# Fewer places for each expert of a mixture of experts, and one more second product that holds its weights

## The chip, the cores and the metric

The kernel runs on one core of a Trainium2 chip. The metric is the device time of one execution in microseconds. Before the change it was 4212.13 us, the median of three runs (4209.02 to 4219.26).

## The reference

One encoder layer over 2048 tokens of width 1024, with 16 meta tokens in front that take part in attention and are dropped at the end. Two groups of attention heads are mixed and added to the tokens with a layer norm. Then each token goes to 4 of 32 experts:

```
logits = h @ w_router + b_router
top_val, top_idx = lax.top_k(logits, 4); gates = softmax(top_val)
# rows sorted by expert, group_sizes = bincount of the choices
hgu = lax.ragged_dot(xs, w_gate_up, group_sizes) + b_gate_up[e]   # 1024 -> 2048
act = clamped_swiglu(hgu)                                         # 1024
out = lax.ragged_dot(act, w_down, group_sizes) + b_down[e]        # 1024 -> 1024
moe = segment_sum(out * gates, tok)
h = layernorm(2**0.25 * h + moe)
```

8192 rows (2048 tokens by 4) are spread over the experts as the router's logits have it, so the experts differ in size. All data are float32.

## The kernel before

The kernel first computes attention and the mixed tokens, then the router, and then runs the experts. This change bears on the experts alone; they begin at about 1646 us.

**Places by rank.** The kernel counts the rows of each expert on the chip and sorts the experts by their counts. The program is fixed, so each rank r has a fixed number of places, `CAPS[r]`, from 512 for the largest to 128 for the smallest five; the expert itself is looked up by rank when its weights are loaded (`job`, L1831). All places are computed, whether a row stands in them or not. What goes beyond an expert's places is done after the 32 jobs by a loop `tc.For_i(0, ni)`, one expert piece of 256 places (`OB`) a turn; `ni` is computed on the chip (`leftover`, L1406) and may be 0.

**A job.** `order` sets the jobs in pairs, a large rank and a small one: 1, 26, 2, 25, 3, 24, 4, 23, 5, 22, 6, 21, 7, 20, 8, 19, 9, 18, 10, 31, 11, 30, 12, 29, 13, 28, 14, 27, 15, 17, and then 16 and 0. The places of a job are cut into tiles of up to 128 rows (`j.tb`). Rows are gathered from HBM by an indirect DMA on GpSimd's queue (`rows`, L1514), turned by TensorE and split into a high and a low part (`turns`, L1522); this is done for the next job during the second product of the one before. Weights come in 12 pieces of 1024 KB a job, 8 of the first product and 4 of the second, each split by ScalarE (high, L1472) and VectorE (low, L1478) some pieces ahead.

Products take three terms: high by high, low by high and high by low. There are three modes, by places n:

- over 248 ("w3"): the first product (`up_ws`, L1580) holds weights and streams n columns; 8 steps, 2 halves, 24 matmuls each (L1590, L1591, L1595);
- 129 to 248 ("w2"): high and low rows stand side by side, so a pass with the high weights streams 2n columns (L1593) and one with the low weights n (L1595), 16 matmuls a half;
- up to 128 ("ts"): rows are held and weights are streamed, 256 columns a matmul (L1560, L1562).

The second product has two forms. `down_ts` (L1765) holds the rows: 4 pieces by tiles, 24 matmuls of 256 columns each (L1773); ScalarE scales the result by the gate into `y`. `down_ws` (L1788) holds the weights and streams the job's columns: 8 blocks of 24 matmuls of n columns (L1803), or 16 of 2n and n columns in w2 (L1799); the result comes out turned, so it is copied, turned back by TensorE tile by tile (L1816) and scaled (L1820). `thin(n)` says which form a job has. When the last piece of a tile's `y` is there, `rows_out` (L1626) adds its rows into the sums `acc_d` in HBM with an indirect scatter on GpSimd's queue. The tool that sets waits makes each scatter wait for the one before.

**The end.** During the last job (rank 0) the kernel normalises all tokens: `norms` (L1689) reads pairs of 128 sums from `acc_d` through SP's queue, takes statistics on VectorE, the root on GpSimd, scales on ScalarE, and shifts on VectorE and GpSimd. Its steps are put between the last job's by the list `TICKS`, in each engine's order. The first read comes in step 0 of the last job and its statistics between steps 1 and 2. The last job's own rows are normalised after their second product (`sums`, `rows_end`), for which GpSimd gathers their sums behind its share of the norms.

Of the kernel before, what the change touches and what calls it, by code (L numbers as in the profile page):

```python
# [48 lines left out]


OB = 256
CAPS = [512, 476, 444, 424, 376, 348, 332, 316, 316, 312, 312, 304, 300, 300, 292, 284,
        264, 244, 244, 232, 216, 212, 208, 200, 200, 188, 160, 128, 128, 128, 128, 128]
MAXI = 8192 // OB + NE

ROOT_BITS = float(0x5f3759df - 2 ** 30 - 2 ** 22)
# [4 lines left out]

def thin(n):

    return 128 < n <= 216 or 256 < n <= 332 or 384 < n < 460


def tables():
# [865 lines left out]
def project(k, a, pre):  # L933
# [16 lines left out]
    with ExitStack() as ctx:  # L950
# [42 lines left out]
        def iota(t, step, base, part):  # L993
            nc.gpsimd.iota(t, pattern=[[step, t.shape[1]]], base=base, channel_multiplier=part,
                           allow_small_or_imprecise_dtypes=True)
# [4 lines left out]
        iota(k.r.spare, 0, S + 1, 1)  # L1000
        for r, c in enumerate(CAPS):
            nc.gpsimd.memset(k.r.crow[:, r:r + 1], float(c))
# [379 lines left out]
def experts(k, a, out):  # L1382
    tc, nc = k.tc, k.nc
    with ExitStack() as ctx:
# [446 lines left out]
        def job(p):  # L1831
            while len(jobs) <= p:
                r = order[len(jobs)]
                j = K()
                j.r, j.n = r, CAPS[r]
                j.mode = "ts" if j.n <= 128 else "w2" if j.n <= 248 else "w3"
                j.dw, j.last = thin(j.n), len(jobs) == NE - 1
                j.e = nc.sync.value_load(k.r.eid[0:1, r:r + 1], min_val=0, max_val=NE - 1)
                j.off = nc.sync.value_load(k.r.off[0:1, r:r + 1], min_val=0, max_val=(NE - 1) * TS)
                j.bias, j.biasa, j.early = k.r.bias[:, :, r], biasa[:, :, r], []  # L1840
                start(j)
                jobs.append(j)
            return jobs[p]
# [214 lines left out]
```

## Time and profile before

| | |
|---|---|
| median of 3 runs | 4212.13 us (4209.02 to 4219.26) |
| profiled execution | 4220.97 us, its span 4219.1 us |
| mean granted TensorE clock | 0.981 of full speed |
| TensorE busy | 4058.6 us (96%) |
| VectorE / ScalarE / GpSimd busy | 2870.7 (68%) / 2386.2 (57%) / 615.9 (15%) |
| HBM read / written | 519.92 / 109.19 MB |

The profile is one execution. Busy times are averages over attention, router, experts and the end, which have different limits. Matmuls overlap, and their ends are modelled; where the price of one matmul matters, the stretch from one start to another is divided by their number.

### The profile page before, as it was taken

How to read it: one execution, taken by the hardware profiler on the slowest of the kernel's cores; microseconds unless marked ns; L12 is line 12 of the kernel's file. 1: busy time of each engine (PE TensorE's matmuls, PEld its weight loads, DVE VectorE, ACT ScalarE, POOL GpSimd, SP SyncE). 2: the span in 40 equal slices, each digit the busy share in tenths (PEclk: the TensorE clock that was granted, in tenths of full speed). 3: DMA queues.
4: the chain of work that ended last, by engine and by line, in shares of the span. 5: the costliest groups of instructions: out<-in, count | busy, mean ns of one | idle time of the engine just before them, and what ended most of it. 6: DMA issues, size and time to landing. Idle time of an engine off the chain costs nothing.

```text
span 4219.1 us, 63411 instructions
## 1 busy us (share of the span) xinstructions
PE 4058.6 (96%) x24294; PEld 3677.9 (87%) x24294; DVE 2870.7 (68%) x4629; ACT 2386.2 (57%) x3847; POOL 615.9 (15%) x547
## 2 busy tenths in 40 slices
PE   8999999999999997999999999999999999999995
PEld 6887777888887776999999999999999999999985
DVE  8876888888887885455554654665655566665665
ACT  5454888866665333455464555565555566665542
POOL 1010011100000341010010100111110011100156
PEclk9999999999999998999999999999999999999997
DMA  5332201111102535465565665766666677776653
GB/s 195 125 124 83 76 28 43 32 37 46 38 29 90 170 112 165 117 199 159 157 195 157 194 188 165 221 194 178 205 200 192 202 243 233 239 222 206 213 189 143
DMA packets 574203, 633.40 MB, mean 150 GB/s; under 512 B 68464, under 2 KB 519664, under 8 KB 573856
## 3 DMA queue, kind: packets, MB, share of 16 engines
q1 hardware_dynamic: 545600, 551.90, 40.6%
q0 software_dynamic: 26528, 75.21, 7.5%
q8 instruction: 195, 3.19, 0.3%
q10 hardware_dynamic: 1760, 2.11, 0.1%
q14 instruction: 120, 0.98, 0.1%
HBM read 519.92 MB, written 109.19 MB: 149 GB/s over the span
## 4 chain that ended last, share of the span: by engine, by line
PE 51%; DMA 5%; DVE 2%; POOL 2%; issue 1%; ACT 1%; POOLq 0%; DVEq 0%; ACTq 0%; SPq 0%
PE dn L1803 9%; PE dn L1773 5%; PE g L1595 5%; PE l L1595 5%; PE g L1590 4%; PE g L1591 4%; PE l L1591 4%; PE l L1590 4%; DMA xg<-h_d,idx 3%; PE g L1593 2%; PE l L1593 2%; PE dn L1799 2%; PE tr L1535 1%; PE g L1560 1%; PE tr L1816 1%
## 5 line engine op out<-in xcount | busy, mean ns | idle before, releaser
L1478 DVE TENSOR_TENSOR wlo<-big,whi 128x2048 fp32r<-128x2048 f32 x384 | 879.3, 2290 | 557.1 <-PE l L1595 267.7
L1472 ACT CAST whi<-big 128x2048 fp32r<-128x2048 f32 x384 | 774.8, 2018 | 30.9 <-DMA big<-in_w_gate_up_dram 17.0
L1628 POOL DMA_INDIRECT acc_d<-y,idx x76 | 156.1, 2054 | 1428.9 <-ACT y L1820 849.4
L1590 PE MATMUL g<-x,whi 128*128 128x316 f32 (+13 forms) x1088 | 338.8, 325 | 2.9 <-DVE ga L1545 2.6
L1591 PE MATMUL g<-x,whi 128*128 128x316 f32 (+13 forms) x1088 | 336.6, 323 | 0.0
L1591 PE MATMUL l<-x,whi 128*128 128x316 f32 (+13 forms) x1088 | 334.9, 321 | 0.0
L1590 PE MATMUL l<-x,whi 128*128 128x316 f32 (+13 forms) x1088 | 334.6, 321 | 0.0
L134 DVE TENSOR_TENSOR pl<-pf,ph 128x1024 fp32r<-128x1024 f32 x256 | 313.3, 1224 | 23.2 <-ACT ph L133 22.8
L735 DVE TENSOR_TENSOR acc<-acc,pf 128x1024 f32<-128x1024 f32 (+1 forms) x224 | 255.5, 1141 | 73.3 <-ACT pf L718 38.7
L1803 PE MATMUL dn<-a,whi 128*128 128x312 f32 (+9 forms) x1664 | 286.8, 314 | 0.0
L1820 ACT ACTIVATE y<-tr,gate 128x128 f32<-128x128 f32 (+14 forms) x440 | 129.0, 362 | 275.6 <-PE tr L1816 275.2
L1595 PE MATMUL g<-x,wlo 128*128 128x244 f32 (+21 forms) x1728 | 278.0, 303 | 0.0
L1595 PE MATMUL l<-x,wlo 128*128 128x244 f32 (+21 forms) x1728 | 278.0, 303 | 0.0
L133 ACT CAST ph<-pf 128x1024 fp32r<-128x1024 f32 x256 | 269.1, 1052 | 6.4
L1603 ACT ACTIVATE li<-l,biasT 128x316 f32<-128x316 f32 (+13 forms) x136 | 74.9, 551 | 339.4 <-PE l L1595 331.8
L1773 PE MATMUL dn<-whi,a 128*128 128x256 f32 (+4 forms) x1600 | 235.8, 291 | 29.6 <-DVE big L1741 18.3
L1595 PEld LDWEIGHTS l<-x,wlo 128*128 128x128 f32 x1728 | 255.2, 189 | 7.1
L1595 PEld LDWEIGHTS g<-x,wlo 128*128 128x128 f32 x1728 | 255.1, 189 | 7.1
L1803 PEld LDWEIGHTS dn<-a,whi 128*128 128x128 f32 x1664 | 249.1, 188 | 2.4
L1773 PEld LDWEIGHTS dn<-whi,a 128*128 128x128 f32 (+4 forms) x1600 | 211.6, 192 | 33.1 <-DVE big L1741 14.3
L1615 ACT CAST a<-ga 128x200 fp32r<-128x200 f32 (+21 forms) x216 | 95.1, 440 | 239.7 <-DVE ga L1548 238.3
L708 PE MATMUL s<-qh,big 128*128 128x512 f32 (+1 forms) x544 | 218.5, 402 | 9.9 <-SPq L562 8.1
(483 smaller groups left out, 9793.7 us busy)
## 6 DMA issues: line engine op xcount, KB each, us to landing
big<-in_w_gate_up_dram SPq DMA_DIRECT2D x256, 1024.0 KB
big<-in_w_down_dram SPq DMA_DIRECT2D x128, 1024.0 KB
xt<-in_x_dram SPq DMA_DIRECT2D x16, 512.0 KB
h_d<-xt SPq DMA_DIRECT2D x16, 512.0 KB
n<-ev SPq DMA_DIRECT2D x32, 256.0 KB
u<-uo SPq DMA_DIRECT2D x32, 256.0 KB
ut<-u SPq DMA_DIRECT2D x8, 1024.0 KB
ht<-h_d SPq DMA_DIRECT2D x8, 1024.0 KB
```

The lines of the kernel that those rows point to most:

```text
L133: k.nc.scalar.copy(hi, src)
L134: k.nc.vector.tensor_sub(lo, src, hi)
L708: nc.tensor.matmul(o, u.kv[0][:, sl], u.qh, start=True, stop=False)
L735: nc.vector.tensor_add(u.acc[:n, :m], u.acc[:n, :m], pf[:n, :m])
L1472: nc.scalar.copy(h, raw)
L1478: nc.vector.tensor_sub(l, raw, h)
L1590: nc.tensor.matmul(pz[:, :n], wh, j.x[:, i, :n], start=i == 0, stop=False)
L1591: nc.tensor.matmul(pz[:, :n], wh, j.x[:, i, n:2 * n], start=False, stop=False)
L1593: nc.tensor.matmul(pz[:, :2 * n], wh, j.x[:, i, :2 * n], start=i == 0, stop=False)
L1595: nc.tensor.matmul(pz[:, :n], w[1][:, i, cs], j.x[:, i, :n], start=False, stop=i == 7)
L1773: nc.tensor.matmul(py, (j.ah, j.al)[p][:, f, t0:t0 + n], w[q][:, f], start=o == 0, stop=o == 23)
L1803: nc.tensor.matmul(py[:, :n], w[q][:, f, ms], (j.ah, j.al)[p][:, f, :n], start=o == 0, stop=o == 23)
```

## The change

Two edits. The list of places by rank gets shorter: rank 0 and the last five ranks keep theirs, ranks 1 to 4 lose 12 each, the others 4 or 8, so that 8,460 places stand in place of 8,656. And `thin` takes in 340, the new size of rank 5, whose second product then holds the weights. Since `thin` goes by size and the mode does too, every other rank has the form that the two functions give for its new size.

```
-CAPS = [512, 476, 444, 424, 376, 348, 332, 316, 316, 312, 312, 304, 300, 300, 292, 284,
-        264, 244, 244, 232, 216, 212, 208, 200, 200, 188, 160, 128, 128, 128, 128, 128]
+CAPS = [512, 464, 432, 412, 364, 340, 324, 308, 308, 304, 304, 296, 292, 292, 284, 276,
+        256, 240, 236, 228, 208, 208, 204, 196, 196, 180, 156, 128, 128, 128, 128, 128]

 def thin(n):
-    return 128 < n <= 216 or 256 < n <= 332 or 384 < n < 460
+    return 128 < n <= 216 or 256 < n <= 340 or 384 < n < 460
```

## Rows read from the trace of the kernel before

**Rows 1.** The page, part 1: busy us, share of the span, instructions.
```profile
PE 4058.6 (96%) x24294; PEld 3677.9 (87%) x24294; DVE 2870.7 (68%) x4629; ACT 2386.2 (57%) x3847; POOL 615.9 (15%) x547
```

**Rows 2.** Waits of PE, 1646 to 4023 us: us in total, times, longest.
```profile
PE tr L1535 <- DMA xg<-h_d,idx: 19.2, 12, 4.3
PE tr L1816 <- DVE ga L1810: 3.6, 6, 0.8
```

**Rows 3.** The page, part 6: issues of the experts' weights.
```profile
big<-in_w_gate_up_dram SPq DMA_DIRECT2D x256, 1024.0 KB
big<-in_w_down_dram SPq DMA_DIRECT2D x128, 1024.0 KB
```

**Rows 4.** Windows: first, second product of ranks 2, 5, 6, 16; second of 17; first of 18, 22, 26.
```profile
core 0: us, PE busy (x) PEld busy (x) DVE busy (x) ACT busy (x) POOL busy (x), PEclk, DMA share, GB/s
1839.79:1917.37 77.58, 77.58 (x389) 72.39 (x387) 34.05 (x41) 29.89 (x35) 7.19 (x4) 1.00 0.45 133
1917.37:1960.79 43.42, 43.42 (x237) 40.13 (x236) 13.32 (x13) 20.13 (x41) 0.00 (x0) 1.00 0.34 98
2374.40:2435.93 61.53, 61.53 (x390) 61.51 (x387) 31.64 (x41) 27.53 (x35) 8.54 (x4) 1.00 0.61 182
2435.93:2472.01 36.08, 36.01 (x306) 35.81 (x305) 13.14 (x12) 15.57 (x21) 1.65 (x1) 1.00 0.41 120
2537.91:2596.33 58.42, 58.42 (x389) 58.41 (x387) 31.22 (x41) 27.31 (x35) 6.46 (x4) 1.00 0.64 191
2596.33:2629.11 32.78, 32.78 (x231) 32.69 (x230) 13.02 (x12) 17.95 (x35) 0.00 (x0) 1.00 0.45 130
3947.54:3994.25 46.71, 46.71 (x389) 46.56 (x387) 29.76 (x44) 25.35 (x31) 7.80 (x3) 1.00 0.72 220
3994.25:4023.05 28.80, 28.80 (x248) 28.64 (x246) 15.11 (x15) 19.29 (x39) 1.87 (x2) 1.00 0.61 192
3922.03:3947.54 25.51, 25.51 (x218) 25.20 (x217) 15.71 (x16) 16.00 (x21) 3.81 (x2) 1.00 0.60 188
3086.05:3129.68 43.63, 43.63 (x262) 39.02 (x260) 31.60 (x54) 26.66 (x43) 9.09 (x5) 1.00 0.76 223
2472.01:2510.34 38.33, 38.33 (x258) 38.18 (x257) 30.43 (x54) 24.19 (x37) 5.79 (x4) 1.00 0.85 251
1780.16:1813.29 33.13, 33.13 (x259) 33.13 (x257) 28.02 (x54) 23.14 (x37) 10.48 (x5) 1.00 0.89 253
```

**Rows 5.** Timeline of PE, rank 26: start us, us, engine, line, op, shapes, count.
```profile
1780.16 1.33 PE L1593 MATMUL g<-x,whi 128*128 128x320 f32 x8
1781.33 1.02 PE L1595 MATMUL g<-x,wlo 128*128 128x160 f32 x8
1782.18 1.38 PE L1593 MATMUL l<-x,whi 128*128 128x320 f32 x8
```

**Rows 6.** Timeline of PE, second product of rank 5.
```profile
2435.93 1.83 PE L1773 MATMUL dn<-whi,a 128*128 128x256 f32 x14
2437.60 1.00 PE L1773 MATMUL dn<-wlo,a 128*128 128x256 f32 x7
```

**Rows 7.** Timeline of POOL: both scatters of rank 17, the first of rank 16.
```profile
3945.69 1.65 POOL L1628 DMA_INDIRECT acc_d<-y,idx  x1 [17.64 <-ACT y L1779]
3953.70 4.21 POOL L1628 DMA_INDIRECT acc_d<-y,idx  x1 [6.36 <-DMA acc_d<-y,idx]
...
4035.25 2.87 POOL L1628 DMA_INDIRECT acc_d<-y,idx  x1 [25.33 <-ACT y L1820]
```

**Rows 8.** The chain that ended last, 4045 to 4060 us: start, us, what.
```profile
4050.33 3.12 DMA acc_d<-y,idx
...
4053.70 3.74 DMA xg<-acc_d
```

**Rows 9.** Timeline of DVE, last job: in brackets the idle time before, and its releaser.
```profile
4057.47 2.58 DVE L1650 BATCH_NORM_STATS2 l2st<-xg 128x6 f32<-128x512 f32 x4 [7.93 <-DMA xg<-acc_d]
...
4146.65 0.48 DVE L1741 SCALAR_TENSOR_TENSOR big<-dn,gate,big 128x256 f32<-128x256 f32 x1 [14.00 <-DMA big<-acc_d,idx]
```

**Rows 10.** Windows, one of the last job.
```profile
4080.00:4100.00 20.00, 19.97 (x88) 16.07 (x86) 19.36 (x24) 10.81 (x14) 18.43 (x26) 1.00 0.60 211
```

## The prediction

> **What bounds the kernel now.** The page comes first: the reader is to see that TensorE is counted busy for 96% of the span [rows 1]. Such a share is an average and its ends are modelled, so the second view is who TensorE waits for in the stretch of the experts' jobs, 1646 to 4023 us: the longest entry is 19.2 us, for gathered rows, in 2377 us [rows 2]. Weights never appear there. The third is the issue list: the weight loads number 256 and 128, that is 32 experts by 8 and by 4 pieces [rows 3], so the loop for tokens beyond an expert's places ran no turn. The fourth is a table by stretch, one line a job's first product or second product [rows 4]. I cut it at the first matmul of each. In every line with three passes TensorE is busy from end to end while VectorE and ScalarE are busy 31% to 67% and the DMA share is 0.34 to 0.72. So here the time of a job is TensorE's, and the question is what one place costs it.
>
> **Price of a place.** A first product has 384 matmuls of n columns (8 steps, 2 halves, 24). Rank 2 with 444 places took 77.58 us, rank 6 with 332 took 58.42 [rows 4]: 19.16 / 112 = 0.171 us a place, 0.446 ns a column. A second product that holds the weights has 192 such matmuls and a turn back of the result. From 43.42 (rank 2) and 32.78 (rank 6) [rows 4], after taking 0.9 us off rank 2 for its fourth tile (8 transposes at 0.11), 9.74 / 112 = 0.087 a place. One that holds the tokens streams 256 weight columns per tile; a place costs it nothing while the tiles stay as many.
>
> The jobs of two passes (up to 248 places) stream 2n columns against the high weights and n against the low ones. Eight of 320 columns started 1.17 us before the next group, 146 ns each, and eight of 160 took 0.85 us, 106 ns each [rows 5], where 160 columns at 0.446 would be 71. So the narrow pass stands on a floor, and only the wide one pays. Stretches give 43.63 (244), 38.33 (208) and 33.13 us (160) [rows 4]: 0.147 a place above 208, 0.108 below.
>
> Here a page of the Trainium skill speaks against the change. "TensorE: Matmul & The Clock Gate", section "Back-to-back issue gap", says that in a stream of weight load and matmul pairs one matmul comes every 81 ns at 128 columns and every 131 ns at 512, which is 0.13 ns a column. An estimate by that page makes the 42 us that parts 1, 2, 4 and 5 below get from columns about 12. The trace differs (202 ns at 444 columns, 152 at 332, by the first two lines named above), and the measurement decides.
>
> **The parts, one by one.**
> 1. First products of ranks 1 to 15 lose 12 places four times and 8 eleven times, 136: 136 x 0.171 = 23.3 us.
> 2. Second products of ranks 2, 3 and 6 to 15, which hold the weights before and after, lose 104 places: 104 x 0.087 = 9.0.
> 3. Rank 5 (348 to 340) changes the operand it holds. Before: 3 tiles x 4 pieces x 24 = 288 matmuls of 256 columns, 36.08 us [rows 4]. After: rank 6's 32.78 + 8 x 0.087 = 33.5. Gain 2.6. ScalarE gets 24 small scalings in place of 12 and all three scatters come at the end; rank 6 carries the same work with ScalarE at 17.95 of 32.78 us [rows 4], so it stays hidden.
> 4. Rank 16 (264 to 256) changes too, though the title doesn't say so: 256 is not over 256, so it now holds the tokens, and it has two tiles in place of three. First product: by the slope 1.4 less, but matmuls of 256 columns elsewhere come every 119 ns (14 in 1.67 us [rows 6]) against 121.6 in its own row, which makes it 1.0. I take 1.0, the nearer row. Second product: 28.80 now; rank 17, which has the coming form, took 25.51 [rows 4] with 24 transposes for its successor, and rank 16 prepares 32, so 26.4: gain 2.4. Rank 17's end loses 8 of those transposes: 0.9. Sum 4.3, from 3 to 5.
> 5. Ranks 17 to 22 down to 208 places lose 28 in the first product: 4.1; ranks 22 to 26 lose 24 below that: 2.6. Ranks 20 to 26 lose 36 in second products with 64 wide passes: 36 x 128 x 0.446 ns = 2.1. Sum 8.8. Their second products are where TensorE waits for the next job's gathers [rows 2]; a shorter second product meets the same gather, so I take off 1 (bounds 0 and 2.1).
>
> Columns and forms: 23.3 + 9.0 + 2.6 + 4.3 + 8.8 - 1.0 = 47 us.
>
> 6. The end. The last job, rank 0 of 512, is not touched, but what it waits for is. Scatters into the sums go one after another. Rank 16 now sends its first at 4035.25, 12.2 us into the last job [rows 7], and its third at 4050.33. Only when that has landed is the first pair of sums read, at 4053.70 [rows 8], and VectorE, whose next instruction in order is that pair's statistics, stands still for 7.93 us [rows 9]. Rank 17, two tiles and the coming form, sends its two at -1.9 and +6.2 us about its successor's start [rows 7]. So rank 16's last scatter goes some 20 us earlier in the last job, and VectorE's wait goes. What is late next? From there VectorE is busy 19.36 of 20 us and GpSimd 18.43 [rows 10] on the norms, and GpSimd's queue ends in the gather of the last rows for which VectorE waits 14.00 us [rows 9], TensorE with it. A queue that full passes an earlier start on to its end. At most 7.9 comes out, at least 0, if TensorE's steps pace the norms instead; I take 7, since full queues are the nearer row.
>
> Sum 47 + 7 = 54 us. It is made against the profiled execution, 4220.97 us with its span of 4219.1; the median of the runs is 4212.13, 8.8 lower. The saved work is the same in both: 4212 - 54 = 4158.
>
> **What the trace can't tell: whether the tokens fit.** [Rows 3] show that no expert had more than its old places. For the new ones I evaluated the reference's own router in float32 on its inputs. By rank the counts are 498, 461, 432, 411, 363, 338, 322, 308, 306, 304, 301, 296, 292, 291, 281, 276, 256, 238, 235, 226, 208, 206, 202, 195, 194, 180, 155, 116, 107, 81, 70, 43. Each fits, and nine are exactly equal to their places. The closest choice between a fourth and a fifth expert that would overfill one has logits 0.0004 apart, where logits spread by about 1.
>
> **Rivals.**
> - A token flips and one expert overflows. The loop then takes one turn of 256 places: at least rank 16's first and coming second product, 46 + 23 = 69 us, and at most its 12 pieces of 1 MB unhidden in front of that, 12.6 MB at the 220 GB/s of rank 16's stretch [rows 4] = 57 more. With 100, 4258 us, slower than before. It decides from one token over. For: nine counts without room. Against: the kernel carries high and low parts through its products, and needs an error of 0.0004. Chance 0.04.
> - The gathers take back what the small jobs win, and the last job is paced by TensorE's steps: parts 1 to 4 less the waits that grow, 39 - 3 = 36 us, 4176. For: gathers are already the only wait. Against: the wait for them is 19.2 us in all over 12 places, and the big jobs, where most is saved, have none. Chance 0.10.
> - The spacing of matmuls follows the weight loads and not the columns, as in the narrow passes [rows 5]: then only forms and end are left, 2.6 + 3.3 + 7 = 13 us, 4199. Against: the slope over 264 to 444 places. Chance 0.02. The page of the Trainium skill named above would lead there; no stretch here agrees with its figure at 512.
> - The change doesn't take effect, for instance because VectorE, ScalarE or DMA sets the pace of a pair of jobs: 4212. Against: none is over 67% busy in the three-pass jobs [rows 4]. Chance 0.01.
>
> **How the numbers follow.** The forecast holds 0.83 of the chance, with a range of its own from 4212 - 65 (all of part 6, part 5 whole, a few us fewer at gathers, runs 3 us low) to 4212 - 42, 4147 to 4170. To leave out no more than 2 in 10 I go to 4145 and 4176, which takes in the second case. 0.3% is 12.6 us, about what a measurement of this kernel tells from none. Faster: 0.83 + 0.10 = 0.93; same: 0.02 + 0.01 = 0.03; slower: 0.04.
>
> **What would show it.** In the changed profile rank 2's first product should take 75.5 us, rank 6's 57.0; rank 5's second product 33.5 with its transposes in it; rank 16's 26.4 with matmuls of 256 columns; the last job should begin some 47 us earlier, near 3976, and the statistics of its first pair should wait for nothing. Weight loads of 264 and 132 would mean that an expert overflowed. A last job that begins later than 3985, or one that still lasts 196 us to the end of the span, would show parts 1 to 5 or part 6 wrong.

## The result and the profile after

The changed kernel took 4148.3 us (median of 5 runs, 4145.89 to 4160.99) against 4213.89 for the kernel before: a ratio of 0.9849, with an interval from 0.9837 to 0.9860, or 59 to 69 us less. The forecast was 54 us less.

The profiled execution took 4160.99 us with a span of 4159.1. First come the stretches of the changed kernel that answer to [rows 4]: first and second product of rank 2, second of rank 23 (which the rows before didn't have), both of ranks 5 and 6, first of rank 18, second of rank 17 and both of rank 16. The columns are those of [rows 4].

```profile
1839.09:1914.69 75.60, 75.60 (x389) 72.53 (x387) 33.74 (x41) 29.72 (x35) 6.76 (x4) 1.00 0.47 143
...
2330.02:2353.57 23.55, 22.74 (x169) 22.24 (x167) 18.09 (x23) 18.07 (x33) 2.42 (x1) 1.00 0.64 203
2353.57:2413.79 60.22, 60.22 (x390) 60.21 (x387) 31.42 (x41) 27.39 (x35) 6.96 (x4) 1.00 0.64 185
2413.79:2447.16 33.37, 33.37 (x231) 33.24 (x230) 12.98 (x12) 17.92 (x35) 0.00 (x0) 1.00 0.42 127
...
2514.08:2570.94 56.86, 56.86 (x389) 56.85 (x387) 31.01 (x41) 27.12 (x35) 7.05 (x4) 1.00 0.66 195
2570.94:2603.15 32.21, 32.21 (x231) 32.15 (x230) 12.96 (x12) 17.92 (x35) 0.00 (x0) 1.00 0.44 133
3051.18:3093.09 41.91, 41.91 (x263) 38.71 (x260) 31.19 (x54) 26.55 (x43) 8.14 (x5) 1.00 0.79 231
3873.10:3897.24 24.14, 24.14 (x210) 24.14 (x209) 15.41 (x14) 15.88 (x19) 1.61 (x1) 1.00 0.61 196
3897.24:3943.80 46.56, 46.56 (x388) 46.41 (x387) 29.57 (x44) 25.05 (x31) 6.77 (x3) 1.00 0.73 220
3943.80:3970.23 26.43, 26.43 (x227) 26.43 (x225) 15.08 (x15) 15.38 (x20) 3.49 (x3) 1.00 0.64 203
```

The reader is to see that a stretch got shorter in the ratio of its columns, that TensorE still fills it, and that the second product of rank 5 now looks like that of rank 6. The last job begins at 3970.23 in place of 4023.05 and lasts 188.9 us to the end of the span in place of 196.1.

What the kernel before showed in rank 23's second product, in the same view:

```profile
2344.06:2374.40 30.34, 25.30 (x168) 24.55 (x167) 18.20 (x23) 18.39 (x33) 2.65 (x1) 0.89 0.51 157
```

Its matmuls went from 200 to 196 places, but it lost 6.8 us, and its mean granted clock rose from 0.89 to 1.00 of 2.4 GHz: some of the stretch had been at 1.2 GHz, after TensorE had stood still. That is no matter of columns but of a wait. The longest waits of TensorE in the experts' jobs of the changed kernel, 1650 to 3970 us, answer to [rows 2]:

```profile
PE tr L1535 <- DMA xg<-h_d,idx: 15.5, 10, 3.7
PE tr L1816 <- DVE ga L1810: 4.4, 9, 0.8
```

The end: GpSimd's scatters of rank 16, and VectorE's first statistics in the experiment that changes rank 16 alone, are shown with that experiment below.

By stretch, from the two profiles (jobs cut at their first matmul):

| part | forecast, us | measured, us |
|---|---|---|
| 1. first products, ranks 1 to 15 | 23.3 | 24.4 |
| 2. second products that hold weights | 9.0 | 9.4 |
| 3. rank 5's form | 2.6 | 2.7 |
| 4. rank 16, with rank 17's end | 4.3 | 3.9 |
| 5a. first products, ranks 17 to 26 | 6.7 | 7.7 |
| 5b. second products, ranks 18 to 26 | 1.1 | 11.1 |
| jobs of 128 places (27 to 31) | 0 | -1.9 |
| 6. last job and end | 7 | 7.2 |

Together 64.5, and 64.9 with the second products of ranks 1 and 4; the spans differ by 60.0, since the profiled execution of the changed kernel came to the experts 4.9 us later (1650.68 us against 1645.78). The surprise stands in 5b. Of its 11.1 us, 6.8 are rank 23's and 4.4 those of ranks 25 and 26; the rest adds up to nothing. The 4.4 can't be put down to the change: rank 25's second product took 26.70 us in this profile and 29.16 in the next one of the same kernel.

### The profile page after: what moved, and what is told of

The parts are those of the page before. It is cut to its first block, busy times and chain, and to the rows that moved or that the text cites. A ratio compares the mean times of both kernels' runs of the same rounds, so it can differ in the third digit from the quotient of the medians.

```text
span 4159.1 us, 63191 instructions
## 1 busy us (share of the span) xinstructions
PE 4007.4 (96%) x24190; PEld 3638.6 (87%) x24190; DVE 2860.4 (69%) x4627; ACT 2378.7 (57%) x3841; POOL 607.9 (15%) x545
## 4 chain that ended last, share of the span: by engine, by line
PE 52%; DMA 3%; DVE 2%; POOL 2%; issue 1%; ACT 1%; POOLq 0%; DVEq 0%; ACTq 0%
PE dn L1803 9%; PE l L1595 5%; PE g L1595 5%; PE dn L1773 5%; PE g L1590 4%; PE g L1591 4%; PE l L1590 4%; PE l L1591 4%; PE l L1593 3%; PE g L1593 3%; PE dn L1799 2%; DMA xg<-h_d,idx 2%; PE tr L1535 1%; PE tr L1816 1%; DVE wlo L1478 1%; DMA acc_d<-y,idx 1%
## 5 line engine op out<-in xcount | busy, mean ns | idle before, releaser
L1590 PE MATMUL g<-x,whi 128*128 128x308 f32 (+13 forms) x1088 | 331.7, 320 | 0.0
L1591 PE MATMUL g<-x,whi 128*128 128x308 f32 (+13 forms) x1088 | 329.8, 319 | 0.0
L1590 PE MATMUL l<-x,whi 128*128 128x308 f32 (+13 forms) x1088 | 328.6, 317 | 0.0
L1591 PE MATMUL l<-x,whi 128*128 128x308 f32 (+13 forms) x1088 | 328.1, 317 | 0.0
L1803 PE MATMUL dn<-a,whi 128*128 128x308 f32 (+9 forms) x1664 | 284.9, 313 | 0.0
L1820 ACT ACTIVATE y<-tr,gate 128x128 f32<-128x128 f32 (+10 forms) x440 | 128.9, 362 | 259.9 <-PE tr L1816 259.7
L1595 PE MATMUL g<-x,wlo 128*128 128x196 f32 (+21 forms) x1728 | 273.3, 300 | 0.0
L1595 PE MATMUL l<-x,wlo 128*128 128x196 f32 (+21 forms) x1728 | 273.3, 300 | 0.0
L1603 ACT ACTIVATE li<-l,biasT 128x308 f32<-128x308 f32 (+13 forms) x136 | 74.0, 544 | 330.4 <-PE l L1595 330.3
L1615 ACT CAST a<-ga 128x196 fp32r<-128x196 f32 (+21 forms) x216 | 93.8, 434 | 240.0 <-DVE ga L1548 238.7
```

Of the source, the lines that this page charges most:

```text
L1590: nc.tensor.matmul(pz[:, :n], wh, j.x[:, i, :n], start=i == 0, stop=False)
L1591: nc.tensor.matmul(pz[:, :n], wh, j.x[:, i, n:2 * n], start=False, stop=False)
L1595: nc.tensor.matmul(pz[:, :n], w[1][:, i, cs], j.x[:, i, :n], start=False, stop=i == 7)
L1803: nc.tensor.matmul(py[:, :n], w[q][:, f, ms], (j.ah, j.al)[p][:, f, :n], start=o == 0, stop=o == 23)
```

## The experiments

Two theories for 5b: **A**, gather waits are a matter of phase and move by some us either way; **B**, fewer places make them shorter as such. A third, **C**, came out of the first four runs.

**The changed kernel again.** No edit.

> The changed kernel once more, for a second profile and more times. Both theories: 60 to 70 us faster than before. Theory A (gather waits are a matter of phase: each gather's landing depends on which weight loads it falls among, so their sum moves by some us from execution to execution and from kernel to kernel, either way): TensorE's waits for gathered rows in single jobs differ from the first profile by several us. Rival B (fewer places make the gather waits shorter as such): the same jobs wait the same, 18 us in all.

4150.6 us, ratio 0.9853 (0.9838 to 0.9868). Rank 23's second product took 23.5 us again, but rank 30's took 15.5 in place of 20.8. So both kinds are there: a wait that a kernel has or hasn't, and one that changes from execution to execution. For the second kind this is GpSimd's timeline around the end of rank 30's first product, in the first profile of the changed kernel:

```profile
3332.91 1.59 POOL L1628 DMA_INDIRECT acc_d<-y,idx  x1 [46.59 <-ACT y L1820]
3341.02 3.35 POOL L1628 DMA_INDIRECT acc_d<-y,idx  x1 [6.51 <-DMA acc_d<-y,idx]
3352.82 2.21 POOL L1628 DMA_INDIRECT acc_d<-y,idx  x1 [8.45 <-DMA acc_d<-y,idx]
3355.33 1.04 POOL L1518 DMA_INDIRECT xg<-h_d,idx  x1 [0.30 <-issue]
```

and in the second:

```profile
3323.69 1.59 POOL L1628 DMA_INDIRECT acc_d<-y,idx  x1 [46.59 <-ACT y L1820]
3330.97 1.56 POOL L1628 DMA_INDIRECT acc_d<-y,idx  x1 [5.68 <-ACT li L1567]
3340.63 1.45 POOL L1628 DMA_INDIRECT acc_d<-y,idx  x1 [8.11 <-DMA acc_d<-y,idx]
3342.39 1.01 POOL L1518 DMA_INDIRECT xg<-h_d,idx  x1 [0.30 <-issue]
```

The same program. In the first, the second scatter started 0.8 us later after the one before and then took 3.35 us in place of 1.56, the third started 11.8 us after it in place of 9.7, and the gather behind them in the queue came 22.4 us after the first scatter in place of 18.7. TensorE's stretch was longer by 5.4. Below, a second scatter of such a three that takes 2.4 us or more is called a slip. What brings it about is not shown.

**Rank 16 alone.**

```
-        264, 244, ...
+        256, 244, ...
```

> Before, with rank 16 alone at 256 places (tokens held, two tiles). Both theories: rank 17's end -1 us, rank 16 -2.5, last job and end -7: 10 to 11 us faster, and VectorE's wait of 7.9 us for the first pair of sums gone. A rival for the end (TensorE's steps pace the norms): 3 to 4 us faster, the last job as long as before.

4203.35 us, ratio 0.9972 (0.9962 to 0.9982): 8 to 16 us faster, 10 by the medians. Its profile has rank 16's parts as the changed kernel has them (46.56 and 26.43 us) and 189.4 us from the last job's start in place of 196.1. GpSimd's scatters at that start, 4012.16 us, and VectorE's first statistics:

```profile
4010.37 1.61 POOL L1628 DMA_INDIRECT acc_d<-y,idx  x1 [10.01 <-ACT y L1779]
4021.84 1.57 POOL L1628 DMA_INDIRECT acc_d<-y,idx  x1 [9.86 <-DMA acc_d<-y,idx]
```

```profile
4038.17 2.47 DVE L1650 BATCH_NORM_STATS2 l2st<-xg 128x6 f32<-128x512 f32 x4
```

The wait of [rows 9] is gone: no bracket stands behind the statistics. Part 6 is right in its place and its mechanism, and near in size (6.7 us here); the rival, in which TensorE's steps pace the norms, falls.

**The small ranks alone** (17 to 26) **and the large ranks alone** (0 to 15, with `thin` up to 340): the new numbers of `CAPS` in one half of the list, the old in the other.

> Before, with the new places of ranks 17 to 26 alone. Columns: 9 us faster. Theory A: 9 us, and up to 7 more or less by gather waits. Rival B: 9 us, since the gathers that TensorE waits for are those of the large ranks, whose rows don't change here; waits for gathers stay at 19 us.

> Before, with the new places of ranks 0 to 15 alone and rank 5 holding the weights. Columns and form: 23.3 + 9.0 + 2.6 = 35 us faster. Theory A: 35, and up to 7 more or less by gather waits. Rival B: the large ranks' gathers have fewer rows, so waits fall by the 7 us that the changed kernel shows: 42 us faster.

4199.65 us, 0.9965 (0.9952 to 0.9979), and 4163.96 us, 0.9879 (0.9864 to 0.9894). So 14 us for the small ranks (9 to 20 by the interval) and 50 for the large ones (44 to 57), each above its columns; the 50 are more than either theory had. In the profile of the large ranks alone rank 23, which still has 200 places, has lost its wait; with the small ranks alone it has 196 places and keeps it. TensorE's waits from 2280 to 2380 us, around rank 23's second product, with the small ranks alone:

```profile
PE tr L1535 <- DMA xg<-h_d,idx: 5.0, 1, 5.0
PE tr L1816 <- DVE ga L1810: 0.8, 1, 0.8
```

large ranks alone:

```profile
PE tr L1816 <- DVE ga L1810: 0.8, 1, 0.8
```

The wait therefore belongs to the rows gathered for rank 5, as B has it. But rank 22's wait for rank 6's rows, of which there are also 8 fewer, did not shrink (1.8 us in the kernel before, 2.6 here; the stretch took 27.57 and 28.33 us). B falls on that. The three parts add up to 73 us where the whole has 63 to 66; what makes the parts better than their columns is said under "right or wrong".

**Theory C.** Part of the answer stands in the counts of packets. A part tile is the last tile of a job, where it has fewer than 128 rows. Lines of the view of DMA queues, for GpSimd's queue while rank 5's third gather is under way (packets, MB, share of 16 engines). The kernel before, 92 rows:

```profile
q0 software_dynamic: 384, 0.38, 10.1%
```

The changed kernel, 84 rows:

```profile
q0 software_dynamic: 112, 0.34, 8.2%
```

92 rows go with 292 small packets beside them, 84 with 28. The packets of all part tiles can be counted so: beyond one a row and 16 more, there are 276 for 92 rows, 228 for 76, 204 for 68, 348 for 116, but 36 for 108, 12 for 84, 4 for 60 and none for 48, 80 and 112. Each is (16 - g) x n / g, where g is the largest divisor of n up to 16: 12 x 23, 12 x 19, 12 x 17, 12 x 29, 4 x 9, 2 x 6, 1 x 4. That looks like n rows spread evenly over g of the 16 DMA engines, with a filler for each row on the idle ones; the counts and the landing times (13.1 us after issue for 92 rows, 7.3 for 84) are measured, the spread itself is inferred, since the trace doesn't say which engine a packet ran on. The times of the packets speak for it: while rank 5's third gather moved, 2.8 of its rows were under way at once on average with 92 rows, and 8.9 with 84. The small packets took 9 ns each, in the middle, and the rows 187. It was tested by gathering more rows without computing more:

```
+            m = -(-n // 16) * 16
-            ... out=xg[:n] ... ap=j.idx[:n, i:i + 1] ...
+            ... out=xg[:m] ... ap=j.idx[:m, i:i + 1] ...
```

> Before, with each gather of a part tile reading up to the next multiple of 16 rows (into places that no product reads); no column of any matmul changes. Theory C (an indirect DMA spreads n rows evenly over the largest number of DMA engines up to 16 that divides n, so 92 = 4 x 23 and 76 = 4 x 19 rows go through 4 engines and land late): rank 23's second product loses its 4.3 us wait for rank 5's third gather, rank 22's most of its 2 us wait for rank 6's; together 4 to 7 us faster. Theory A (phase alone): no change beyond 2 us either way, the 4.3 us wait stays at its place.

4194.92 us, ratio 0.9959 (0.9947 to 0.9972), 17 us faster with 96 and 80 rows gathered in place of 92 and 76. Rank 23's second product fell from 30.34 to 23.74 us, rank 22's from 27.57 to 23.95. Of TensorE's timeline in rank 23's second product, the transposes of rank 5's third tile; the kernel before:

```profile
2361.41 0.85 PE L1535 MATMUL tr<-ident,xg 92*128 92x92 f32 x4 [4.25 <-DMA xg<-h_d,idx]
```

the same with padded gathers (one line further down in the code):

```profile
2345.07 0.48 PE L1536 MATMUL tr<-ident,xg 92*128 92x92 f32 x4
```

and its queue, now with 96 rows and 16 packets:

```profile
q0 software_dynamic: 112, 0.39, 8.3%
```

More bytes, sooner there (with 96 rows 10.5 are under way at once): C holds for these two gathers and B is out. The two stretches are 10 us shorter, the waits themselves 6 of them; the rest is TensorE at the lower clock after a wait (0.89 and 0.94 on average in the kernel before, 1.00 here). C had 4 to 7 us for the whole; the other 7 of the 17 it doesn't explain. In the two profiles the second products of ranks 29 and 31 alone differ by 7.7 us, as they also do between executions of one kernel.

> The changed kernel with its gathers of part tiles read up to the next multiple of 16 rows. Theory C: only rank 6's third gather of 68 = 4 x 17 rows is waited for; rank 22's second product gets 2 to 3 us shorter, the kernel 1 to 4 us faster than the changed one, so 67 to 70 us faster than before. Theory A: as the changed kernel.

4150.6 us, ratio 0.9845 (0.9832 to 0.9858). Rank 22's second product went from 28.57 to 23.80 us, 4.8 where C had 2 to 3 (it took 26.71 in the other profile of the changed kernel), and rank 6's 68 rows no longer hold it up. The whole time doesn't tell the two kernels apart; 4 us are below what these runs resolve. Besides, this profile loses 5.1 us where no gather is left: from GpSimd's last scatter into the output to the end of the span it has 15.1 us in place of 10.0, because the engine's closing DRAIN takes 7.3 us in place of 3.2 and the semaphore increment before it 2.0 in place of 1.0.

The other way round, only rank 5's third gather of the changed kernel is made bad again:

```
+            m = 92 if j.r == 5 and i == 2 else n
```

> The changed kernel, with rank 5's third gather alone reading 92 rows in place of 84; no column changes. Theory C: the wait of 4 to 5 us in rank 23's second product is back (28 us and over in place of 23.6), the kernel 4 to 5 us slower than the changed one, 60 us faster than before. Theory A: 23.6 us, as the changed kernel.

4152.37 us, ratio 0.9850 (0.9837 to 0.9863). The wait is back at its place: rank 23's second product takes 28.19 us, and its queue shows the 384 packets again. The transposes that waited in the kernel before, and the queue while the gather is under way:

```profile
2346.21 0.79 PE L1536 MATMUL tr<-ident,xg 84*128 84x84 f32 x4 [3.00 <-DMA xg<-h_d,idx]
```

```profile
q0 software_dynamic: 384, 0.38, 10.1%
```

This is the experiment that shows the cause: 8 rows more in one gather, which no product reads, bring back 4.6 of the 6.8 us; in the six other profiles of the new places with gathers the stretch took 23.5 us each time. In the whole time the kernel is 4 us over the changed kernel's first median, 2 over its second, inside the noise.

**An overflow.** Rank 25, whose expert has 180 rows, gets 176 places.

> The changed kernel with 176 places for rank 25, whose expert has 180 rows, so that the loop behind the jobs takes one turn. By the price of the rival: 69 to 126 us more than the changed kernel, 4217 to 4275 us, and weight loads of 264 and 132 in place of 256 and 128.

4272.97 us in one run, 125 over the changed kernel's median and near the upper end of the price, but not by its terms. The loop begins its first product 195.6 us after the last job's start, where the changed kernel was done after 188.9. That product took 48.3 us with TensorE busy throughout, so its eight loads were hidden. From there 75.0 us go to the end of the span, with loads of the second product's pieces, a scatter and the norms of the extra rows on the chain. The weight loads:

```profile
big<-in_w_gate_up_dram SPq DMA_DIRECT2D x264, 1024.0 KB
big<-in_w_down_dram SPq DMA_DIRECT2D x136, 1024.0 KB
```

I had expected 132: the loop loads each of the 4 pieces of the second product once for each of its two tiles. In the changed kernel the numbers are 256 and 128; no expert overflowed there.

**Without gathers.** In both kernels the gather of every job after the first becomes a fill by GpSimd.

```
-            nc.gpsimd.indirect_dma_start(out=xg[:n], ... in_=k.h1_d, ...)
+            nc.gpsimd.memset(xg[:n], 0.5)
```

> Before, with the gather of every job after the first replaced by a GpSimd fill of the same tile with 0.5 (left out: the tokens of the experts' rows). TensorE's waits for gathered rows go, 16 to 21 us: about 4194 us. If the forecast's terms are right and only gather waits were misjudged (theory C for rank 5's gather, A for the rest), this kernel and the next differ by columns and forms 48 plus the end 7, 55 us; if places cost more than the forecast had, by 62 to 66, as before and changed kernel do.

> The changed kernel with the same gathers replaced by a fill (left out: the tokens of the experts' rows). Right terms and misjudged gather waits: 55 us below the kernel before with its gathers replaced, about 4139. Places dearer than forecast: 62 to 66 below it, 4128 to 4132.

4204.14 us (0.9970, 0.9959 to 0.9980) and 4141.98 (0.9823, 0.9809 to 0.9836). Without gathers the kernel before gains 8 to 17 us, 13 by the medians, where 16 to 21 were expected; the fills have a price of their own, since the first products of the jobs of 128 places take 28.6 to 29.1 us in place of 27.6 in both kernels, some 6 us in all. The two are 62 us apart, which by the words of the expectation speaks for dearer places. The stretches say otherwise. From the first job's start to the last's, and from there on; the kernel before without gathers:

```profile
1642.58:4000.36 2357.78, 2340.56 (x16207) 2277.06 (x16208) 1407.72 (x1877) 1321.36 (x2036) 213.64 (x147) 1.00 0.61 182
4000.36:4195.00 194.64, 143.81 (x774) 125.83 (x772) 126.18 (x194) 63.50 (x84) 125.85 (x181) 0.88 0.48 166
```

the changed one:

```profile
1644.31:3953.39 2309.08, 2290.33 (x16107) 2239.18 (x16107) 1394.20 (x1876) 1314.80 (x2035) 216.22 (x147) 1.00 0.62 186
3953.39:4139.00 185.61, 142.31 (x771) 125.07 (x769) 126.17 (x194) 62.84 (x78) 121.22 (x179) 0.88 0.50 174
```

48.7 us in the jobs, where the forecast had 48 before its deduction, and 8 to 9 at the end. But the execution of the first that was profiled was its fastest of eight (4196.91), and where its other executions are slower no profile shows. So places cost what was forecast, in the stretches; the last 5 us of this pair stay open.

**Tokens held by rank 5.** The changed kernel with `256 < n <= 332` as before.

> The changed kernel with the second edit undone: rank 5 of 340 places holds its tokens in the second product. By part 3 its second product takes 36.1 us in place of 33.4, the kernel 2.7 us more than the changed one, 60 to 63 us faster than before. Rival (the form costs ScalarE and GpSimd time elsewhere, so it gives nothing in all): the same time as the changed kernel, with other stretches shorter by as much.

4144.94 us, ratio 0.9826 (0.9813 to 0.9839). Its second product takes 35.93 us, 2.6 more than with weights held, as forecast, yet the whole is not slower; it is faster by 0.2%, with intervals that just touch. Once more, with padded gathers:

> The new places, rank 5 holding its tokens, and gathers of part tiles read up to the next multiple of 16 rows. If the 2.6 us of rank 5's form are a gain that the whole keeps (part 3): 2 to 3 us slower than the same with weights held, 60 to 63 us faster than before. If the form gives nothing in all (the rival of the run before, which came out at 0.9826): 70 to 75 us faster than before. Theory C: no wait over 2 us for the gathers of ranks 5 and 6. Theory A: 128-place jobs take about 16 us in their second product, or 20 to 22 where the second scatter ahead starts later than 15.6 us before it.

4151.81 us, ratio 0.9839 (0.9826 to 0.9853), 68 us faster than before and beside 0.9845 for weights held. So the second edit wins its 2.6 us in its place, and no time of the whole shows it. In both profiles with tokens held no job of 128 places had a slip, and their five second products took 15.6 to 16.6 us; the five profiles of the new places with weights held and all gathers present (the changed kernel twice, padded, with 92 rows, with the overflow) had one or two slips each. Whether the form does that or chance does, seven profiles can't tell. The one with padded gathers has the long closing of the padded run above (15.1 us after the last scatter), so its time holds 5 us that belong to no gather and no product. None of these versions beats the changed kernel clearly.

## Why the prediction was right, and where it was not

The range held the time and the sign was right; the size was 10 us short. The lower edge of the range took in "a few us fewer at gathers", but no reason for fewer was given, so that 4148 lies inside it is in part luck.

- **Price of a place, parts 1 to 3, 5a.** Right within 1.2 us each. The bound, TensorE from end to end of a three-pass job, and the price read from two stretches carried almost all of the forecast. 5a is right in its sum only: rank 22's first product gained nothing for 4 places and rank 25's 1.55 us for 8. The rival in which matmuls follow the weight loads falls: rank 2's 75.60 us and rank 6's 56.86 are those of the slope. What the Trainium skill states ("TensorE: Matmul & The Clock Gate", section "Back-to-back issue gap"), 81 ns a matmul at 128 columns and 131 at 512, doesn't hold for these matmuls: the two stretches make 197 ns at 432 columns and 148 at 324. An estimate by that page makes part 1 about 7 us, where 24.4 were measured, and the whole about 24 us (54 - 42 + 12), where the prediction lets it lead to the rival's 13.
- **Part 4.** Rank 16's first product gained 0.15 us in place of 1.0: at 256 columns it stands at 121.3 ns a matmul (46.56 / 384), against 121.6 at 264. Neither the slope nor the 119 ns of [rows 6] held there. Rank 17's end gave 1.4 in place of 0.9, of which 1.1 with rank 16 changed alone.
- **Part 6.** Right, 7.2 against 7, 0.9 of them behind the last scatter. The reason given, a queue full to its end passes an earlier start on, held in every profile: GpSimd's last scatter into the output came 183.8 to 185.5 us after the last job's start in the five with rank 16 at 264, and 177.0 to 179.4 in the nine with 256, 6.4 less on average. What follows it took 9.0 to 10.9 us where no loop's turn comes, but for the two with padded gathers of the new places, where GpSimd's closing made it 15.1; why it is longer there is open.
- **Part 5b failed, in its sign.** The step was "a shorter second product meets the same gather, so I take off 1". It was not the same gather. Rank 5's third tile went from 92 to 84 rows, and rank 23's second product lost 6.8 us. The wait of 19.2 us in [rows 2] was read as a price that stays, without asking which of the 12 gathers it was made of and what the new places do to each. The last gather of the first job, rank 1 (92 to 80 rows, nothing hides it), adds some 2 us: from its issue to the first product 9.1 to 10.9 us in four profiles with 92 rows, 7.2 to 8.7 in nine with 80. That this is theory C again is not shown: the padded kernel before, with 96 rows there, took 9.7.
- **The rest is phase, as far as it is known.** The 128-place jobs wait for their gathers behind three scatters. In 60 such second products of twelve profiles, ten had the second of those scatters take 2.4 us or more, and took 18.5 to 22.0 us; of the other 50, one took 19.4 and the rest 15.2 to 17.1. The kernel before, the part changes and the padded gathers of before had none or one of these slips, the changed kernel two and one. That is part of why the parts add up to more than the whole, and likely of why its runs lie between 4145 and 4161; the second is argued, since only the profiled executions show their slips.

Columns and forms 48, end 7, rank 5's gather 6.4 and rank 1's 2 make 63 to 64; the whole shows 59 to 69.

## What to carry to other kernels

Where one engine fills a stage, the price of a unit of work is the slope between two stretches of that stage, and it forecasts well, here from 444 columns down to 276; at 256 it no longer held. What doesn't follow from it is a wait at the border, whose size depends on the exact counts: list each wait by itself, and ask what the change does to the transfer behind it. Where an engine waits for an indirect DMA, give it a number of rows with a divisor near 16 (84 = 14 x 6 was as good as 96), or pad it, before counting the rows it saves.

## What was not expected of the hardware

An indirect DMA of 92 rows of 4 KB landed 13.1 us after its issue, one of 84 rows 7.3 and one of 96 rows 6.8, all beside weight loads; a scatter of 92 rows took 15.8 us to its last packet, one of 84 rows 7.4. Fewer rows can be slower and more rows faster. And a scatter that started 0.8 us later in one execution than in another went with a stretch of TensorE that was 5 us longer two steps down the same queue.
